# A hybrid decoder trunk on one core: squares summed on VectorE, 512-column query, key and output-gate products, and gate projections stacked into one fp32r pass

## The chip, the core and the metric

The program runs on one core of a Trainium2 chip. TensorE (PE) multiplies matrices and adds up in PSUM, VectorE (DVE) and ScalarE (ACT) do elementwise work, GpSimd (POOL) a little of it, and SyncE's queue (SP) issues the transfers. Each engine runs its own list of instructions in order and waits by semaphores. The metric is the device time of one execution in microseconds, as a median over runs.

## The reference, cut to what matters

The trunk has two layers on x of 256 tokens by 2048 channels: a convolution module and a feed-forward network (FFN), then gated linear attention and a second FFN. Around each of the four sub-layers stand an RMS norm, a modulation by a conditioning vector c (`w_ada`: six chunks of 2048 per layer) and a second RMS norm on its output. The change touches the attention and the place of some `w_ada` tiles:

```python
def gla_mixer(h, w_in, w_gate_up, b_gate, norm_g, w_out):
    proj = h @ w_in
    q, k, v, r, a = jnp.split(proj, [...])      # 1024, 1024, 2048, 2048, 16 columns
    g = jax.nn.log_sigmoid((a @ w_gate_up + b_gate).astype(jnp.float32)) / GLA_GATE_TAU
    ...
    _, o = lax.scan(step, S0, (qc, kc, vc, gc))  # chunks of 64 tokens, 4 heads
    o = rms_norm(o, norm_g.reshape(GLA_HEADS, GLA_HEAD_V))
    o = o.reshape(bsz, L, GLA_DV).astype(h.dtype) * jax.nn.silu(r)
    return o @ w_out
```

Each of the four heads has 256 columns of q and k and 512 of v and o. The norm of o takes the mean of squares over the 512 columns of one head and one token.

## The kernel before

Activations stand transposed, channels on the 128 partitions and tokens along the free dimension. A weight matrix is cut into 128x128 blocks. Sixteen blocks make a tile of 1 MB, which one transfer on SP's queue brings into a `raw` buffer (six of them, L321). Each half of a tile, eight blocks, is split: ScalarE casts it to fp32r as `hi` (L326), VectorE subtracts to get the rest, `lo` (L327). Three halves are prepared ahead of the one in use. A product of a block with an activation pair x_hi, x_lo is hi times x_hi, hi times x_lo and lo times x_hi. `product()` does this in three ways: "packed", two blocks in one bank, three matmuls of 256 columns (L368 to L370); "narrow", three of 256 columns into one half of a bank (L392, L393, L398); and wide, one of 512 columns over x_hi and x_lo side by side (L395) and one of 256 (L398). A wide result stands in two halves of a bank that have to be added: `joined` has ScalarE copy one (L410) and VectorE add the other (L411).

The order of tiles is a list (`tile_order`, L90): the weight tiles of the stages, with the tiles of `w_ada` spread among them. A `w_ada` tile, an "ada" tile below, goes through the same buffers, but VectorE alone uses it: one multiplication with a sum along the row over 128x2048 elements (L303). `EARLY` says how many ada tiles of one chunk, `scale2`, stand in the first FFN; the rest stand in the stages v, r and wo of the attention. Which instruction of an engine stands behind which is set by a scheduler at build time, from the order of the code and its own plan of times; the engines then keep to it.

Between two sub-layers stands a `junction` (L524): sums over channels by TensorE (`sum_sq`, L418: fp32, two passes per matmul, one result column, for each half of the tokens), then 1/sqrt on GpSimd and VectorE, a matmul that spreads it over the partitions, the new x, and the modulation into h. A few matmuls (`fill`) run in its pauses. The junction j1 leads from the first FFN into the attention. Its sums end with those of the last output block: f_y, f_z (squares on ScalarE) and f_xz (a product on VectorE, L515).

The attention (L823 to L982) has these stages:

- aqk: 17 blocks of columns: the 16 gate columns first (padded to 128), then q and k by head. The first eight are computed side by side ("packed", over half of the rows), the nine after that "narrow". When the gate block is done, `gates()` (L839) makes the decays: eight products z in fp32 from `wgu` (16x1024, loaded at L831) and `at` (16x256), each with an Abs on ScalarE (L845) and an addition with a minimum on VectorE (L846); then an Exp (L849) and a Ln (L850) over 128x2048, a subtraction on VectorE (L851), eight running sums (L853). After that `level`, `merge` and `diagonal` work off the scores by head, some in the v stage.
- v: the value columns.
- `attend(h)` (L947): per head four blocks of o (L953, L954). ScalarE squares each (L956), VectorE copies it (L957), and `sum_sq` adds it over channels on TensorE, into one result per head (`sso`). Then 1/sqrt, its spreading (`no_rb`), and the scaling of o.
- r: 16 narrow blocks. `r_done` takes silu, multiplies with o, splits into `oo`.
- wo: 16 blocks over `oo`, 15 of them wide; then the junction j2.

Of the kernel before, what the change touches and what calls it, by code (L numbers as in the profile page):

```python
# [7 lines left out]
F32 = mybir.dt.float32  # L8
F32R = mybir.dt.float32r
I8 = mybir.dt.int8  # L10
AF = mybir.ActivationFunctionType
ALU = mybir.AluOpType
PSUM = bass.MemoryType.PSUM

P = 128
D = 2048
KD = D // P
T = 256
# [6 lines left out]
DK = 1024  # L25
KK = DK // P
RANK = 16
EPS = 1e-6
HEAD = 8
TILE = 16  # L30
HALF = 8
LEAD = 8
EARLY = 4
CRITICAL = 3000
FILL = 8
TBUFS = 5
# [98 lines left out]
def trunk(ctx: ExitStack, tc: tile.TileContext, a: dict, out: bass.AP):  # L135
    nc = tc.nc
# [5 lines left out]
    tmp = ctx.enter_context(tc.tile_pool(name="tmp", bufs=2))  # L142
# [48 lines left out]
    inv_e = const.tile([P, 1], F32, tag="inv_e", name="inv_e")  # L191
# [7 lines left out]
    h = const.tile([P, KD, 2, T], F32R, tag="h", name="h")  # L199
    h_hi, h_lo = h[:, :, 0, :], h[:, :, 1, :]  # L200
    s_y = const.tile([P, T], F32, tag="s_y", name="s_y")
# [216 lines left out]
    def sum_sq(ssp, sq, w, first, last):  # L418
        for t in range(2):
            ends["sum"] = nc.tensor.matmul(  # L420
                ssp[:, t : t + 1], sq[:, t * P : (t + 1) * P], w,
                start=first and t == 0, stop=last, skip_group_check=True,
            ).ins

    def new_ss(name):
        return ps2.tile([P, 512], F32, tag="ss", name=name)
# [27 lines left out]
    def new_sq(name):  # L454
        return tmp.tile([P, T], F32, tag="sq", name=name, bufs=3)
# [22 lines left out]
    def square_into(total, src, name, first, **kw):  # L478
        if first:
            nc.scalar.activation(out=total, in_=src, func=AF.Square, **kw)  # L480
            return
        sq = new_sq(name)
        nc.scalar.activation(out=sq, in_=src, func=AF.Square, **kw)
        nc.vector.tensor_tensor(out=total, in0=total, in1=sq, op=ALU.add)
# [338 lines left out]
    with tc.tile_pool(name="gla", bufs=1) as gp:  # L823
# [3 lines left out]
        nc.gpsimd.memset(sc1, 0.0)  # L827
        vt = y.rearrange("p (t k) n -> p t (k n)", t=2)
        with tc.tile_pool(name="scores", bufs=1) as sp:
            wgu = sp.tile([RANK, DK], F32, tag="wgu", name="wgu")  # L830
            nc.sync.dma_start(out=wgu, in_=a["wgu"])  # L831
            at = sp.tile([P, T], F32, tag="at", name="at")
            bc = sp.tile([P, KK, T], F32, tag="bc", name="bc")
            gm = y[:, :KK, :]
            keep = sp.tile([P, T], F32, tag="keep", name="keep")
            nc.gpsimd.memset(keep, 1.0)
# [2 lines left out]
            def gates():  # L839
                nc.scalar.preload_act_table_set("natural_log_exp_and_others")  # L840
                for j in range(KK):
                    z = ps2.tile([P, 512], F32, tag="acc", name=f"z{j}", bufs=2)[:, :T]
                    nc.tensor.matmul(z, wgu[:, j * P : (j + 1) * P], at[:RANK, :], start=True, stop=True)
                    bg = col("gla_b_gate", j)
                    nc.scalar.activation(out=bc[:, j, :], in_=z, func=AF.Abs, bias=bg)  # L845
                    nc.vector.tensor_scalar(  # L846
                        out=gm[:, j, :], in0=z, scalar1=bg, scalar2=0.0, op0=ALU.add, op1=ALU.min
                    )
                nc.scalar.activation(out=bc, in_=bc, func=AF.Exp, scale=-1.0)  # L849
                nc.scalar.activation(out=bc, in_=bc, func=AF.Ln, bias=1.0)  # L850
                nc.vector.tensor_tensor(out=gm, in0=gm, in1=bc, op=ALU.subtract)  # L851
                for j in range(KK):
                    nc.vector.tensor_tensor_scan(  # L853
                        out=bc[:, j, :], data0=keep, data1=gm[:, j, :], initial=0.0, op0=ALU.mult, op1=ALU.add
                    )
# [36 lines left out]

            def aqk_done(ob, acc):
                if ob == 2 * KK:
                    nc.scalar.copy(at[:RANK, :], acc[:RANK, :])
                    gates()
                    return
                h = (ob % KK) // 2
                if h not in qk:
                    qk[h] = [  # L900
                        sp.tile([P, 2, T], F32, tag=tag, name=f"{tag}{h}", bufs=HEADS) for tag in ("q", "k")
                    ]
                which = ob // KK
                nc.scalar.activation(
                    out=qk[h][which][:, ob % 2, :], in_=acc, func=AF.Copy, scale=1.0 if which else 0.0625
                )
                if which and ob % 2:
                    work.extend((h, s) for s in (128, 64, 32, 16, 8, 4, 2, 1, 0))
# [7 lines left out]
                        else:  # L916
                            diagonal(h)

            product("aqk", KD, h_act, aqk_done, step, narrow=range(2 * KK + 1), packed=HEAD * KD)

            accs = {}
            for idx, (ob, k) in enumerate(ORDERS["v"]):
# [20 lines left out]
        with tc.tile_pool(name="og", bufs=1) as op:  # L943
            oo = op.tile([P, KD, 2, T], F32R, tag="oo", name="oo")
            on = {}

            def attend(h):  # L947
                ssp = new_ss(f"sso{h}")[:, :2]
                o = [op.tile([P, T], F32, tag="o", name=f"o{h}{j}", bufs=6) for j in range(4)]
                for j in range(4):  # L950
                    e = slice((4 * h + j) * P, (4 * h + j + 1) * P)
                    po = ps2.tile([P, 512], F32, tag="acc", name=f"po{h}{j}", bufs=2)[:, :T]
                    nc.tensor.matmul(po, vt[:, 0, e], sc0[:, h, :], start=True, stop=False)  # L953
                    nc.tensor.matmul(po[:, P:], vt[:, 1, e], sc1[:, h, :], start=False, stop=True)  # L954
                    sq = new_sq(f"o_sq{h}{j}")
                    nc.scalar.square(sq, po)  # L956
                    nc.vector.tensor_copy(o[j], po)  # L957
                    sum_sq(ssp, sq, inv_e, j == 0, j == 3)
                rbo = rstd(ssp, f"no{h}")
                for j in range(4):  # L960
                    nc.vector.scalar_tensor_tensor(
                        out=o[j], in0=o[j], scalar=col("gla_norm_g", 4 * h + j), in1=rbo,
                        op0=ALU.mult, op1=ALU.mult,
                    )
                on[h] = o

            def r_done(ob, acc):
                sr = tmp.tile([P, T], F32, tag="t", name=f"sr{ob}", bufs=TBUFS)
                nc.scalar.activation(out=sr, in_=acc, func=AF.Silu)
                nc.vector.tensor_tensor(out=sr, in0=sr, in1=on[ob // 4][ob % 4], op=ALU.mult)  # L970
                gather_x(ob, "w")
                split(sr, oo[:, ob, 0, :], oo[:, ob, 1, :])
                if ob % 4 == 1 and ob // 4 + 1 < HEADS:
                    attend(ob // 4 + 1)

            attend(0)
            product("r", KD, h_act, r_done, narrow=range(KD))

            def wo_done(ob, acc):
                gather(ob, "w", acc, kind=5)  # L980

            product("wo", KD, lambda k: oo[:, k, :, :], wo_done, narrow=(KD - 1,))  # L982
# [110 lines left out]
```

## Time and profile before

| | before |
|---|---|
| median of 3 runs | 2414.77 us (2414.39 to 2417.88) |
| profiled execution | 2412.25 us |
| its span, first to last instruction | 2410.5 us |
| mean granted TensorE clock (share of full) | 0.986 |
| busy: TensorE / its weight loads / VectorE / ScalarE / GpSimd | 98% / 85% / 73% / 46% / 1% |
| moved from and to the chip's memory | 605.27 MB, 251 GB/s on average |

The span begins with the first instruction of the program and ends with the last; the execution's time is 1.75 us longer. Times in the trace count from the span's start. The first FFN runs from about 452 to 1194 us, the junction j1 to 1206, aqk to 1325, v to 1437, r to 1545, wo to 1634, the junction j2 to 1647. Matmuls are pipelined, so that the durations of neighbours overlap. What one costs is read from start to start, or from the number of matmuls in a window that they fill.

### The profile page before, as it was taken

How to read it: one execution, taken by the hardware profiler on the slowest of the kernel's cores; microseconds unless marked ns; L12 is line 12 of the kernel's file. 1: busy time of each engine (PE TensorE's matmuls, PEld its weight loads, DVE VectorE, ACT ScalarE, POOL GpSimd, SP SyncE). 2: the span in 40 equal slices, each digit the busy share in tenths (PEclk: the TensorE clock that was granted, in tenths of full speed). 3: DMA queues.
4: the chain of work that ended last, by engine and by line, in shares of the span. 5: the costliest groups of instructions: out<-in, count | busy, mean ns of one | idle time of the engine just before them, and what ended most of it. 6: DMA issues, size and time to landing. Idle time of an engine off the chain costs nothing.

```text
span 2410.5 us, 36312 instructions
## 1 busy us (share of the span) xinstructions
PE 2353.3 (98%) x14672; PEld 2051.8 (85%) x14672; DVE 1763.6 (73%) x2490; ACT 1110.1 (46%) x1659; POOL 23.9 (1%) x27
## 2 busy tenths in 40 slices
PE   7899999999999999999999999999999999999997
PEld 4677688998888888888899889989888888888886
DVE  5776669887776687779877978898666555666665
ACT  4333345554444444444455444454444444444442
POOL 0000000000000000000000000000000000000001
PEclk8999999999999999999999999999999999999998
DMA  9987978368777788778743666774565665665651
GB/s 390 392 341 277 345 272 336 134 244 300 287 286 285 290 307 293 292 283 295 269 158 127 245 253 252 283 274 140 204 216 209 222 217 208 224 214 208 223 184 65
DMA packets 85027, 605.27 MB, mean 251 GB/s; under 512 B 9574, under 2 KB 9958, under 8 KB 12022
## 3 DMA queue, kind: packets, MB, share of 16 engines
q1 hardware_dynamic: 84858, 602.95, 68.6%
q8 instruction: 115, 1.88, 0.3%
q14 instruction: 54, 0.43, 0.0%
HBM read 600.81 MB, written 2.10 MB: 250 GB/s over the span
## 4 chain that ended last, share of the span: by engine, by line
PE 94%; DVE 2%; DMA 2%; ACT 1%; issue 1%; POOL 0%; SPq 0%; POOLq 0%; ACTq 0%
PE in L395 25%; PE out L395 13%; PE in L398 12%; PE out L398 7%; PE pw L729 3%; PE pw L724 3%; PE pw L730 2%; PE wo L395 2%; PE r L392 1%; PE r L393 1%; PE r L398 1%; PE in_pair L369 1%; PE wo L398 1%; PE in_pair L368 1%; PE in_pair L370 1%; PE v L934 1%
## 5 line engine op out<-in xcount | busy, mean ns | idle before, releaser
L327 DVE TENSOR_TENSOR lo<-raw,hi 128x1024 fp32r<-128x1024 f32 x754 | 920.5, 1223 | 520.5 <-ACT hi L326 515.8
L326 ACT CAST hi<-raw 128x1024 fp32r<-128x1024 f32 x754 | 790.3, 1050 | 1048.9 <-issue 295.0
L395 PE MATMUL in<-h,hi 128*128 128x512 f32 x2560 | 900.1, 398 | 0.1
L398 PE MATMUL in<-h,lo 128*128 128x256 f32 x2560 | 716.7, 280 | 0.0
L395 PEld LDWEIGHTS in<-h,hi 128*128 128x128 f32 x2560 | 481.0, 188 | 117.8 <-DVE gate L799 0.3
L398 PEld LDWEIGHTS in<-h,lo 128*128 128x128 f32 x2560 | 483.4, 189 | 0.0
L395 PE MATMUL out<-m,hi 128*128 128x512 f32 x1364 | 477.3, 395 | 0.0
L398 PE MATMUL out<-m,lo 128*128 128x256 f32 x1408 | 392.2, 281 | 0.0
L303 DVE SCALAR_TENSOR_TENSOR raw<-raw,cb 128x2048 f32<-128x2048 f32 x160 | 365.2, 2284 | 12.1 <-DMA raw<-in_w_ada_dram 12.0
L395 PEld LDWEIGHTS out<-m,hi 128*128 128x128 f32 x1364 | 255.0, 188 | 58.4
L398 PEld LDWEIGHTS out<-m,lo 128*128 128x128 f32 x1408 | 264.4, 188 | 1.9
L724 PE MATMUL pw<-hi,h 128*128 128x512 f32 x256 | 101.3, 417 | 7.0 <-ACT h L467 6.7
L729 PE MATMUL pw<-lo,h 128*128 128x512 f32 x256 | 106.2, 417 | 1.2 <-DVE lo L327 1.2
L730 PE MATMUL pw<-hi,h 128*128 128x512 f32 x256 | 94.0, 395 | 0.0
L395 PE MATMUL wo<-oo,hi 128*128 128x512 f32 x240 | 83.7, 394 | 0.0
L398 PE MATMUL r<-h,lo 128*128 128x256 f32 x256 | 73.3, 286 | 0.0
L392 PE MATMUL r<-h,hi 128*128 128x256 f32 x256 | 73.2, 286 | 0.0
L393 PE MATMUL r<-h,hi 128*128 128x256 f32 x256 | 73.0, 285 | 0.0
L398 PE MATMUL wo<-oo,lo 128*128 128x256 f32 x256 | 71.2, 281 | 0.0
L369 PE MATMUL in_pair<-h,hi 128*128 128x256 f32 x256 | 70.9, 284 | 0.0
L370 PE MATMUL in_pair<-h,lo 128*128 128x256 f32 x256 | 68.9, 283 | 0.0
L368 PE MATMUL in_pair<-h,hi 128*128 128x256 f32 x256 | 68.0, 284 | 0.0
(363 smaller groups left out, 2939.1 us busy)
## 6 DMA issues: line engine op xcount, KB each, us to landing
raw<-in_in_dram SPq DMA_DIRECT2D x176, 1024.0 KB, 5.0
raw<-in_w_ada_dram SPq DMA_DIRECT2D x160, 1024.0 KB, 5.2
raw<-in_out_dram SPq DMA_DIRECT2D x88, 1024.0 KB, 5.0
raw<-in_pw_dram SPq DMA_DIRECT2D x48, 1024.0 KB, 7.7
raw<-in_w_ada_r_dram SPq DMA_DIRECT2D x32, 1024.0 KB, 8.3
raw<-in_aqk_dram SPq DMA_DIRECT2D x17, 1024.0 KB, 5.1
raw<-in_v_dram SPq DMA_DIRECT2D x16, 1024.0 KB, 5.0
raw<-in_r_dram SPq DMA_DIRECT2D x16, 1024.0 KB, 6.6
```

Source lines behind the costliest of these rows:

```text
L303: nc.vector.scalar_tensor_tensor(out=raw, in0=raw, scalar=1.0, in1=cb, op0=ALU.mult, op1=ALU.mult, accum_out=modcol(name, i))
L326: nc.scalar.copy(hi, part)
L327: done = nc.vector.tensor_tensor(out=lo, in0=part, in1=hi.bitcast(F32), op=ALU.subtract)
L369: nc.tensor.matmul(acc, w_hi, x_lo, start=False, stop=False, skip_group_check=True)
L370: nc.tensor.matmul(acc, w_lo, x_hi, start=False, stop=closes, skip_group_check=True)
L392: nc.tensor.matmul(acc[:, :T], w_hi[:, s], x_hi, start=n == 0, stop=False)
L393: nc.tensor.matmul(acc[:, :T], w_hi[:, s], x_lo, start=False, stop=False)
L395: nc.tensor.matmul(acc, w_hi[:, s], pair.rearrange("p a b -> p (a b)"), start=n == 0, stop=end, skip_group_check=True)
L398: nc.tensor.matmul(acc[:, :T], w_lo[:, s], x_hi, start=False, stop=end, skip_group_check=ob not in narrow)
L724: nc.tensor.matmul(accs[c][t], h_hi[:, k, n], w_hi[:, s], start=k == 0, stop=False)
L729: nc.tensor.matmul(accs[c][t], h_hi[:, k, n], w_lo[:, s], start=False, stop=False)
L730: nc.tensor.matmul(accs[c][t], h_lo[:, k, n], w_hi[:, s], start=False, stop=k == KD - 1)
```

## The change

There are four parts.

1. `EARLY` goes from 4 to 12: eight ada tiles move from the stages v, r and wo into the first FFN.
2. The gate projection's operands are stacked. `wgu` has 96 rows: the 16 rows of the weight stand at rows 0, 32 and 64, zeros between. They come by a transfer of 384 KB into the memory of `bc`, ScalarE casts all to fp32r, VectorE replaces the last group by the rest. The gate block of aqk has its columns three times, so `at` has 96 rows, of which the second group is replaced by its rest. One fp32r matmul over 96 rows then adds hi times hi, hi times rest and rest times hi.
3. aqk (the nine blocks that are not packed) and r lose `narrow`: they are wide, and joined. `sr` takes the place of the joined tile.
4. In `attend` the squares of a head's four blocks are added in `s_y` or `s_z` by `square_into` (a Square on ScalarE and, after the first, an add on VectorE), and one `sum_sq` per head follows.

```diff
-EARLY = 4
+GATE_ROWS = 32
+GATE_K = 3 * GATE_ROWS
+EARLY = 12
...
-            wgu = sp.tile([RANK, DK], F32, tag="wgu", name="wgu")
-            nc.sync.dma_start(out=wgu, in_=a["wgu"])
-            at = sp.tile([P, T], F32, tag="at", name="at")
             bc = sp.tile([P, KK, T], F32, tag="bc", name="bc")
+            gate_up = bc[:GATE_K, :, :].rearrange("p a b -> p (a b)")[:, :DK]
+            nc.sync.dma_start(out=gate_up, in_=a["wgu"])
+            wgu = sp.tile([GATE_K, DK], F32R, tag="wgu", name="wgu")
+            nc.scalar.copy(wgu, gate_up)
+            low = slice(2 * GATE_ROWS, GATE_K)
+            nc.vector.tensor_tensor(out=wgu[low, :], in0=gate_up[low, :], in1=wgu[low, :].bitcast(F32), op=ALU.subtract)
+            at = sp.tile([GATE_K, T], F32R, tag="at", name="at")
...
-                    nc.tensor.matmul(z, wgu[:, j * P : (j + 1) * P], at[:RANK, :], start=True, stop=True)
+                    nc.tensor.matmul(z, wgu[:, j * P : (j + 1) * P], at, start=True, stop=True)
...
-                    nc.scalar.copy(at[:RANK, :], acc[:RANK, :])
+                    nc.scalar.copy(at, acc[:GATE_K, :])
+                    low = slice(GATE_ROWS, 2 * GATE_ROWS)
+                    nc.vector.tensor_tensor(out=at[low, :], in0=acc[low, :], in1=at[low, :].bitcast(F32), op=ALU.subtract)
                     gates()
...
-            product("aqk", KD, h_act, aqk_done, step, narrow=range(2 * KK + 1), packed=HEAD * KD)
+            product("aqk", KD, h_act, aqk_done, step, packed=HEAD * KD)
...
             def attend(h):
-                ssp = new_ss(f"sso{h}")[:, :2]
+                total = (s_y, s_z)[h % 2]
...
-                    sq = new_sq(f"o_sq{h}{j}")
-                    nc.scalar.square(sq, po)
+                    square_into(total, po, f"o_sq{h}{j}", j == 0)
                     nc.vector.tensor_copy(o[j], po)
-                    sum_sq(ssp, sq, inv_e, j == 0, j == 3)
+                ssp = new_ss(f"sso{h}")[:, :2]
+                sum_sq(ssp, total, inv_e, True, True)
...
-                sr = tmp.tile([P, T], F32, tag="t", name=f"sr{ob}", bufs=TBUFS)
+                sr = acc
...
-            product("r", KD, h_act, r_done, narrow=range(KD))
+            product("r", KD, h_act, r_done)
...
-    aqk[:, 2 * DK : 2 * DK + RANK] = w_in[:, 2 * DK + 2 * D :]
+    gate_up = np.zeros((GATE_K, DK), w_in.dtype)
+    for at in range(0, GATE_K, GATE_ROWS):
+        aqk[:, 2 * DK + at : 2 * DK + at + RANK] = w_in[:, 2 * DK + 2 * D :]
+        gate_up[at : at + RANK] = f["gla_w_gate_up"][0]
```

Two lines more stand at the top of the changed kernel, so that a line there has a number two higher up to the attention. VectorE in the junction j1, before: j_r and f_xz belong to its chain, lo is the rest of a weight half.

```order
L327 TENSOR_TENSOR lo_10550<-raw_10547,hi_10549 128x1024
L508 TENSOR_SCALAR y<-y,der 128x256
L535 TENSOR_SCALAR j_r_10606<-j_my 128x2
L515 TENSOR_TENSOR f_xz_10585<-y,x 128x256
L435 TENSOR_TENSOR j1y_dg<-ident,j1y_r_10608 128x256
```

VectorE at the same place of the changed kernel:

```order
L329 TENSOR_TENSOR lo_10574<-raw_10571,hi_10573 128x1024
L523 TENSOR_TENSOR s_xz<-s_xz,f_xz_10522 128x256
L510 TENSOR_SCALAR y<-y,der 128x256
L537 TENSOR_SCALAR j_r_10630<-j_my 128x2
L838 TENSOR_TENSOR wgu<-bc,wgu 32x1024
L517 TENSOR_TENSOR f_xz_10609<-y,x 128x256
L437 TENSOR_TENSOR j1y_dg<-ident,j1y_r_10632 128x256
```

The subtraction of the gate weights (L838) now stands between j_r and f_xz. ScalarE there, in the changed kernel:

```order
L328 CAST hi_10573<-raw_10571 128x1024
L504 ACTIVATE f_y_10606<-y 128x256
L836 CAST wgu<-bc 96x1024
L521 ACTIVATE f_z_10611<-y 128x256
L482 ACTIVATE s_xx<-x 128x256
```

The cast of the gate weights (L836) stands between f_y and f_z, which were neighbours. VectorE in the gate chain of aqk, before: L851 is the subtraction after the logarithm, L853 the eight running sums.

```order
L327 TENSOR_TENSOR lo_11416<-raw_11413,hi_11415 128x1024
L327 TENSOR_TENSOR lo_11420<-raw_11413,hi_11419 128x1024
L851 TENSOR_TENSOR y<-y,bc 128x2048
L327 TENSOR_TENSOR lo_11491<-raw_11488,hi_11490 128x1024
L853 SCALAR_TENSOR_TENSOR bc<-keep,y 128x256 x8
L327 TENSOR_TENSOR lo_11495<-raw_11488,hi_11494 128x1024
```

The same place of the changed kernel:

```order
L329 TENSOR_TENSOR lo_11544<-raw_11541,hi_11543 128x1024
L413 TENSOR_TENSOR join_12_11567<-aqk_11524,join_12_11567 128x256
L857 TENSOR_TENSOR y<-y,bc 128x2048
L329 TENSOR_TENSOR lo_11548<-raw_11541,hi_11547 128x1024
L329 TENSOR_TENSOR lo_11604<-raw_11601,hi_11603 128x1024
L859 SCALAR_TENSOR_TENSOR bc<-keep,y 128x256 x8
L413 TENSOR_TENSOR join_13_11627<-aqk_11584,join_13_11627 128x256
L329 TENSOR_TENSOR lo_11608<-raw_11601,hi_11607 128x1024
```

One rest of a weight half has moved from ahead of the subtraction to behind it, and joins stand between.

## Rows read from the trace of the kernel before

**Rows 1.** Page, section 4: the chain that ended last, by engine.

```profile
PE 94%; DVE 2%; DMA 2%; ACT 1%; issue 1%; POOL 0%; SPq 0%; POOLq 0%; ACTq 0%
```

**Rows 2.** Windows (aqk, r, wo, FFN0): length, busy us of PE, PEld, DVE, ACT, POOL; PEclk; DMA, GB/s.

```profile
1253.50:1325.50 72.00, 69.14 (x538) 65.84 (x538) 53.89 (x96) 41.45 (x72) 0.00 (x0) 0.98 0.39 132
...
1436.70:1544.60 107.90, 107.90 (x883) 107.09 (x882) 88.95 (x139) 53.43 (x92) 4.14 (x4) 1.00 0.71 260
1544.60:1634.40 89.80, 89.80 (x533) 79.29 (x531) 81.29 (x132) 47.32 (x78) 0.00 (x0) 1.00 0.75 272
452.00:1190.00 738.00, 737.93 (x4347) 649.66 (x4346) 587.37 (x748) 350.24 (x506) 0.00 (x0) 1.00 0.78 283
```

**Rows 3.** Groups by line and shape: busy us, mean ns of one, idle before.

```profile
L327 DVE TENSOR_TENSOR lo<-raw,hi 128x1024 fp32r<-128x1024 f32 x754 | 920.5, 1223 | 520.5 <-ACT hi L326 515.8 <-PE ada L255 2.7
L326 ACT CAST hi<-raw 128x1024 fp32r<-128x1024 f32 x754 | 790.3, 1050 | 1048.9 <-issue 295.0 <-PE in L395 240.6 <-PE out L395 227.6
L303 DVE SCALAR_TENSOR_TENSOR raw<-raw,cb 128x2048 f32<-128x2048 f32 x160 | 365.2, 2284 | 12.1 <-DMA raw<-in_w_ada_dram 12.0
...
L411 DVE TENSOR_TENSOR join<-in,join 128x256 f32<-128x256 f32 x160 | 66.7, 417 | 0.0
...
L420 PE MATMUL sso<-inv_e,o_sq 128*128 128x1 f32 x64 | 7.8, 235 | 0.0
```

**Rows 4.** Short windows: steady r, steady wo, then aqk behind its longest wait.

```profile
1520.00:1540.00 20.00, 20.00 (x168) 19.95 (x167) 17.34 (x22) 9.27 (x14) 0.00 (x0) 1.00 0.74 269
1560.00:1580.00 20.00, 20.00 (x116) 17.47 (x115) 19.25 (x29) 10.72 (x18) 0.00 (x0) 1.00 0.90 331
...
1289.50:1292.90 3.40, 3.40 (x18) 3.40 (x18) 3.40 (x6) 1.97 (x6) 0.00 (x0) 0.50 0.68 280
1293.00:1296.40 3.40, 3.40 (x30) 3.40 (x30) 2.55 (x6) 1.60 (x3) 0.00 (x0) 1.00 0.89 301
```

**Rows 5.** Timeline of TensorE at a z product: start us, us, engine, line, work.

```profile
1262.78 0.28 PE L398 MATMUL aqk<-h,lo 128*128 128x256 f32 x1
1262.99 0.69 PE L843 MATMUL z<-at,wgu 16*128 16x256 f32 x2
1263.61 0.39 PE L392 MATMUL aqk<-h,hi 128*128 128x256 f32 x1
1263.83 0.28 PE L393 MATMUL aqk<-h,hi 128*128 128x256 f32 x1
```

**Rows 6.** Timeline of TensorE around eight passes of a head's sums.

```profile
1453.53 0.95 PE L420 MATMUL sso<-inv_e,o_sq 128*128 128x1 f32 x8
1454.34 0.36 PE L393 MATMUL r<-h,hi 128*128 128x256 f32 x1
1454.54 0.28 PE L398 MATMUL r<-h,lo 128*128 128x256 f32 x1
```

**Rows 7.** Timeline of the junction j1, all engines.

```profile
1194.55 0.33 SPq L831 DMA_DIRECT2D wgu<-in_wgu_dram  x1
...
1197.08 0.43 DVE L515 TENSOR_TENSOR f_xz<-y,x 128x256 f32<-128x256 f32 x1
...
1197.57 1.01 PE L420 MATMUL j_m<-two_d,f_xz 128*128 128x1 f32 x4 [1.06 <-DVE f_xz L515]
```

**Rows 8.** Transfers: count, KB each, median us from issue to landing.

```profile
out_dram<-x SPq DMA_DIRECT2D x8, 256.0 KB, 2.0
...
wgu<-in_wgu_dram SPq DMA_DIRECT2D x1, 64.0 KB, 4.8
```

**Rows 9.** Timeline of VectorE in the gate chain.

```profile
1278.99 2.29 DVE L851 TENSOR_TENSOR y<-y,bc 128x2048 f32<-128x2048 f32 x1 [2.00 <-ACT bc L850]
...
1282.33 4.76 DVE L853 TENSOR_TENSOR_SCAN bc<-keep,y 128x256 f32<-128x256 f32 x8
```

**Rows 10.** Timeline of TensorE there: the two waits.

```profile
1282.47 0.39 PE L398 MATMUL aqk<-h,lo 128*128 128x256 f32 x1 [0.44 <-DVE lo L327]
...
1288.26 0.39 PE L398 MATMUL aqk<-h,lo 128*128 128x256 f32 x1 [2.43 <-DVE lo L327]
```

More of the change, by code (lines that the diff above doesn't have):

```diff
@@ L1075 @@
     arr["wo"] = tiles(f["gla_w_out"][0], "wo")
-    arr["wgu"] = np.ascontiguousarray(f["gla_w_gate_up"][0])
+    arr["wgu"] = gate_up
     for l in range(2):
```

## The prediction

> **What bounds the kernel now.** I read the chain of waits first: TensorE holds 94% of the chain that ended last [rows 1]. So only time that TensorE loses or is given can move the end, and other engines count where TensorE waits for them. Next the windows by stage [rows 2]: the reader is to see that the matmuls fill the r, wo and FFN0 stages to the last 0.1 us, and that only aqk has idle time on TensorE, 72.00 - 69.14 = 2.86 us. The short windows [rows 4] give the pitch, which is the window over the number of matmuls: a matmul row's own duration (0.28 us in the timeline) overlaps the next one's and is no cost. The timelines then give the price of the small matmuls between the weight products [rows 5, 6], the end of FFN0, where TensorE has nothing else to do [rows 7], and the gate chain, where it waits for VectorE [rows 9, 10].
>
> **Wide products for aqk and r.** 9 aqk blocks and 16 r blocks of 16 products each, 25 x 16 = 400 pairs, change from three 256-column matmuls to one of 512 columns and one of 256. Three narrow ones take 3 x 20.00/168 = 0.357 us, a wide pair 2 x 20.00/116 = 0.345 [rows 4]; the difference is 0.012. Over the whole wo stage the pair comes to 0.350 (89.80 less 48 narrow matmuls at 0.119, over 240 pairs [rows 2]), against the 0.360 that the steady pitch of 0.12 gives [rows 5]: 0.010. I take 0.011, so 4.4 us, with bounds of 0.009 and 0.014 a pair: 3.6 to 5.6. The joins that this adds (an ACT copy and a VectorE add of 0.417 us per block [rows 3]) lie beside matmuls, apart from the two places below.
> The Trainium skill, "TensorE: Matmul & The Clock Gate", Back-to-back issue gap, speaks against this term: its isolated gap for a full clock is N/2.4 + 2.5 ns, so an estimate from it is three narrow at 109 ns = 328 against 216 + 109 = 325 ns, and the sum would gain 1.1 us here instead of 4.4. The trace does not agree: the narrow matmul's 0.119 us lies above that gap and the pair's 0.345 lies 0.012 below three of them.
>
> **Gate projections.** Eight z products of two passes each become one fp32r pass of 256 columns with 96 rows. Today a z holds TensorE from 1262.99 to 1263.61, 0.62 us, and the matmul before it and the one after it take 0.21 and 0.22 to the next start where 0.12 is normal [rows 5]. If a pass of 0.12 replaces only the 0.62, 0.50 is saved; if both slow starts go too, 0.69. I take 0.54, near the lower end since another shape is loaded either way: 8 x 0.54 = 4.3 us (4.0 to 5.5).
>
> **Squares summed on VectorE.** Sixteen sum pairs of two passes each, 64 passes [rows 3], become four, 16 passes. Eight passes take 1453.53 to 1454.34, 0.81 us, and the next matmul starts slow, 0.2 us [rows 6]: 0.101 to 0.115 a pass. At 0.108 the 48 passes that go are worth 5.2 us (4.8 to 5.5). VectorE gets 12 adds of 0.417.
>
> **What it costs at the end of FFN0.** The order of VectorE and ScalarE puts the new cast and subtraction of the gate weights into the chain of the junction: the subtraction stands ahead of f_xz, for which TensorE waits (1.06 us idle before j_m [rows 7]). Nothing covers TensorE there. The transfer is issued at about 1194.5 as now (it waits for the tiles of FFN0). A 256 KB transfer takes 2.0 us to land [rows 8]; 128 KB more at the 283 GB/s of FFN0 [rows 2] is 0.46, so it lands at about 1197.0. Then the cast, 1.05, and a subtraction as long as one of 1024 columns, 1.22 [rows 3], with some 0.1 between: f_xz starts at 1199.35 where it started at 1197.08, +2.3 us. The bounds are a landing 0.6 earlier (+1.7) and one after 4.8 us, as the 64 KB transfer had today [rows 8] (+4.6). On SP the seventh aqk tile now stands behind this transfer; six are ahead of it, and at 16 x 0.357 = 5.7 us each it is not used until some 34 us after the stage begins, so its delay costs nothing; were it late, its price would be its delay less those 34.
>
> **The gate chain.** Today TensorE is idle 0.44 and 2.43 us for lo tiles behind the log-sigmoid subtraction (2.29) and the eight scans (4.76) [rows 9, 10]; that is the 2.86 of the stage. After it runs at half clock: 18 matmuls in the 3.4 us where 30 go at full [rows 4], 12 x 0.113 = 1.4 us. The new order has one lo, a join, the subtraction, two lo, the scans, a join, a lo. One lo feeds 8 pairs, 2.8 us, and the next product's first matmul (0.2) needs no lo. From the first lo's end to the second's: 0.42 + w + 2.29 + 1.22, where w is what the subtraction waits for the logarithm; less 3.0 that is 0.9 + w. From the second's to the fourth's: 1.22 + 4.76 + 0.42 + 1.22 = 7.6, less two feeds, 5.8: 1.8. Together 2.7 + w against 2.9 now. w is 2.00 today [rows 9], behind one lo more, but with z sooner; I take 0.5: +0.3. Bounds: all stalls gone, -2.9, and w near 3, +3; the half clock may go (-1.4) or come twice (+1.4). The new 32-row subtraction for `at` (about 0.4) delays z, not TensorE, which has aqk blocks to work on.
>
> **Starts of r and wo.** Head 0's attention moves from the end of v into r, and its result is needed by the first r block's product. The row of its scaling stands five halves into r, so I take +0.5 for some late VectorE work (0 to 2.5, the length of one gate-sized wait [rows 10]). The last oo tile comes a copy, a join and some of an ada later, about 1.5 us; the first wo block's last product has some nine instructions of the second block ahead of it, 9 x 0.172 = 1.6: +0.5 (0 to 2).
>
> **Eight ada tiles to FFN0.** 8 x 2.284 = 18.3 us of VectorE [rows 3] move to a stage where it is busy 587.37 of 738.00 and TensorE is full [rows 2]: 0.82 afterwards. I take 0; at worst each holds up one lo, 8 x 1.22 = 9.8; nothing can be gained there, nor in r and wo, where TensorE does not wait now. In r, VectorE gets 16 joins and 12 adds, 28 x 0.417 = 11.7, and loses about four ada tiles, 9.1: the cover of the joins stays.
>
> **Sum.** 4.4 + 4.3 + 5.2 = 13.9 gained; 2.3 + 0.3 + 0.5 + 0.5 = 3.6 lost; net 10.3. The profiled execution took 2412.25 us (span 2410.5), so 2401.95 by its time; it lies 2.5 below the median of 2414.77, against which the forecast stands: 2404.5.
>
> **Rivals.**
> A, the sum above, 2404.5, its own range 2401 to 2407.5.
> B, the waits eat more: the gate weights land after 4.8 us (+4.6) and the gate chain waits with w near 3 and a second half-clock stretch (+4.4). 13.9 - 4.6 - 4.4 - 1.0 leaves 3.9: 2410.9, in milder forms from 2408, with late r and wo starts as well 2413. For it: VectorE is the releaser in both stalls today [rows 10]. Against: a 256 KB transfer landed in 2.0.
> C, slower: VectorE becomes what paces r. The stage wants 107.90 - 2.8 - 5.2 = 99.9 us, VectorE has 88.95 + 2.6 = 91.6 of work in it, a share of 0.917. It decides from the share at which lo tiles come late. If VectorE, waiting for casts, can't be over today's 0.824 [rows 2], r takes 111.1, 3.2 longer than before; the rest, 5.9 gained (13.9 - 8.0) and 3.6 lost, leaves 2415.7, and if waits in each of the four heads bring a half-clock stretch of 1.4 us, 2421. Against: in wo VectorE is busy 0.905 of the stage and 19.25 of 20.00 us in one window, with TensorE full [rows 2, 4].
> D, better: the reordered gate chain lets lo tiles run ahead, and the stalls and the half clock go (-4.3), with r and wo on time: 13.9 - 2.3 + 4.3 = 15.9: 2398.9. For it: two lo stand together between subtraction and scans.
> E, the wide operand does nothing: columns and not instructions set the pitch, a pair costs what three narrow matmuls cost. 13.9 - 4.4 - 3.6 = 5.9: 2408.9. For it: in r a pair has 768 columns either way. Against: the two pitches of [rows 4]. By the page's figures above it would be 2407.8.
>
> **Chances.** A 0.50, B 0.22, C 0.07, D 0.17, E 0.04. No change is within 0.2%, 4.8 us, about what a measurement of this kernel can tell: 2409.9 to 2419.6. Faster: A, D, three quarters of E and a third of B, 0.77. Within: the rest of B and E, 0.16. C I put wholly to slower, 0.07. The range 2400 to 2411 holds A, E, half of D and two thirds of B.
>
> **What would show it.** The r window per pair at 0.345 to 0.350 with VectorE near 0.92 and no wait of TensorE (A, against C and E); z matmuls without the 0.62; 16 sum passes for the heads; f_xz 2 to 3 us later against the last FFN0 matmul; and the gate chain's waits at about 3 us. I am wrong if r's matmuls wait for lo, if f_xz is over 4 us late, or if FFN0 is longer than its 738 us.

## The result, and the profile after

The changed kernel takes 2400.68 us (median of 4 runs, 2395.94 to 2404.08) where the kernel before takes 2415.51 in the same session: the ratio is 0.9936 with a 95% interval of 0.9916 to 0.9956. Between the medians that is 14.8 us less. Measured again in another session (e1 below) it is 2401.16 against 2413.82, ratio 0.9949 (0.9935 to 0.9962). The forecast was 2404.5, 10.3 below the median it started from, with a range of 2400 to 2411 and a chance of 0.77 for faster.

The profiled execution took 2395.94 us, 16.31 less than that of before. Where that lies is read from the starts of the matmuls that open and close each stage. FFN0 and FFN1 are the first and the second FFN, j1 and j2 the junctions in front of aqk and behind wo:

| us | before | after | difference |
|---|---|---|---|
| to the first matmul of FFN0 | 452.32 | 451.86 | -0.46 |
| FFN0 | 741.92 | 741.71 | -0.21 |
| junction j1 | 11.83 | 15.34 | +3.51 |
| aqk, v, r, wo | 428.06 | 414.58 | -13.48 |
| junction j2 | 13.30 | 11.99 | -1.31 |
| FFN1 | 745.37 | 741.51 | -3.86 |
| rest | 17.69 | 17.17 | -0.52 |

The terms of the sum lie in j1 and in aqk to wo: -9.97 against the -10.3 forecast. The forecast did not speak of the two others with a size, FFN1 and j2. Inside aqk to wo, the time from each matmul's start to the next one's start (its pitch), added up by tile, changed by these amounts: aqk -4.3, z -3.8, sums of squares (`sso`) -4.7, r -2.8, v +0.6, wo +1.5.

The chain that ended last, after the change, for [rows 1]: TensorE still binds, VectorE has one percent more.

```profile
PE 93%; DVE 3%; DMA 2%; ACT 1%; issue 1%; POOL 0%; SPq 0%; POOLq 0%; ACTq 0%; DVEq 0%
```

The windows after for [rows 2]: aqk from its first block that is not packed, r, wo, FFN0; the columns are those of [rows 2].

```profile
1255.20:1313.40 58.20, 55.73 (x326) 48.05 (x325) 42.10 (x64) 38.99 (x64) 0.00 (x0) 1.00 0.48 166
1430.00:1532.20 102.20, 102.20 (x594) 90.05 (x593) 90.86 (x159) 58.30 (x109) 4.03 (x4) 1.00 0.66 242
1532.30:1623.50 91.20, 90.42 (x532) 79.19 (x531) 79.29 (x135) 48.37 (x81) 0.00 (x0) 1.00 0.67 247
452.00:1190.00 738.00, 737.93 (x4348) 649.64 (x4348) 602.75 (x760) 349.81 (x505) 0.00 (x0) 1.00 0.79 295
```

r keeps TensorE full with VectorE at 90.86 of 102.20, 0.89, so rival C is out. wo has 0.78 us of idle time that it did not have before. FFN0 carries its extra ada tiles (VectorE 602.75, where the forecast adds up to 605.7) without a loss.

The junction after, which answers to [rows 7]: start, duration, engine, line.

```profile
1193.88 0.33 SPq L834 DMA_DIRECT2D bc<-in_wgu_dram  x1
...
1197.62 1.04 ACT L836 CAST wgu<-bc 96x1024 fp32r<-96x1024 f32 x1 [2.46 <-DMA bc<-in_wgu_dram]
...
1198.70 1.22 DVE L838 TENSOR_TENSOR wgu<-bc,wgu 32x1024 fp32r<-32x1024 f32 x1 [1.96 <-ACT wgu L836]
1199.95 0.43 DVE L517 TENSOR_TENSOR f_xz<-y,x 128x256 f32<-128x256 f32 x1
...
1200.43 1.01 PE L422 MATMUL j_m<-two_d,f_xz 128*128 128x1 f32 x4 [2.33 <-DVE f_xz L517]
```

It takes 3.74 us from the issue of the transfer to the cast's start. Then come cast, subtraction and f_xz, one behind the other, as the forecast had them. f_xz starts 6.38 us after the last matmul of FFN0 (at 1193.57); before the change it was 2.84. That is +3.5 where +2.3 was forecast.

A z product after, for [rows 5], and the sums of one head, for [rows 6]:

```profile
1258.48 0.40 PE L397 MATMUL aqk<-h,hi 128*128 128x512 f32 x1
1258.72 0.40 PE L849 MATMUL z<-at,wgu 96*128 96x256 f32 x2
1258.96 0.28 PE L400 MATMUL aqk<-h,lo 128*128 128x256 f32 x1
...
1443.76 0.50 PE L422 MATMUL sso<-inv_e,s_y 128*128 128x1 f32 x4
```

Two z (`x2` merges two neighbours in one row) take 0.24 us together, and no slow start stands beside them. The four passes of `sso` are all that a head's sums take now.

The gate chain on VectorE after, for [rows 9], and the waits of TensorE, for [rows 10]:

```profile
1285.72 2.29 DVE L857 TENSOR_TENSOR y<-y,bc 128x2048 f32<-128x2048 f32 x1 [1.93 <-ACT bc L856]
1287.93 2.35 DVE L329 TENSOR_TENSOR lo<-raw,hi 128x1024 fp32r<-128x1024 f32 x2
1290.20 4.76 DVE L859 TENSOR_TENSOR_SCAN bc<-keep,y 128x256 f32<-128x256 f32 x8
1294.88 0.40 DVE L413 TENSOR_TENSOR join<-aqk,join 128x256 f32<-128x256 f32 x1
1295.20 1.22 DVE L329 TENSOR_TENSOR lo<-raw,hi 128x1024 fp32r<-128x1024 f32 x1
```

```profile
1287.94 0.50 PE L397 MATMUL aqk<-h,hi 128*128 128x512 f32 x1 [0.18 <-ACT hi L328]
1289.21 0.39 PE L400 MATMUL aqk<-h,lo 128*128 128x256 f32 x1 [0.77 <-DVE lo L329]
...
1296.47 0.39 PE L400 MATMUL aqk<-h,lo 128*128 128x256 f32 x1 [1.43 <-DVE lo L329]
```

TensorE is idle 2.38 us here, before 2.87, but in shorter pieces: two lo tiles now stand between the subtraction and the scans, where one stood. And the half clock of [rows 4] is gone (granted clock 1.00):

```profile
1294.80:1298.20 3.40, 1.97 (x12) 1.55 (x11) 3.40 (x7) 2.86 (x4) 0.00 (x0) 1.00 0.21 39
1298.20:1301.60 3.40, 3.31 (x19) 2.65 (x18) 3.40 (x7) 3.26 (x9) 0.00 (x0) 1.00 0.65 275
```

### The profile page after: what moved, and what is told of

The parts are those of the page before. It is cut to its first block, busy times and chain, and to the rows that moved or that the text cites. A ratio compares the mean times of both kernels' runs of the same rounds, so it can differ in the third digit from the quotient of the medians.

```text
span 2394.2 us, 35471 instructions
## 1 busy us (share of the span) xinstructions
PE 2337.7 (98%) x14216; PEld 2021.1 (84%) x14216; DVE 1775.1 (74%) x2529; ACT 1116.5 (47%) x1685; POOL 23.7 (1%) x27
## 4 chain that ended last, share of the span: by engine, by line
PE 93%; DVE 3%; DMA 2%; ACT 1%; issue 1%; POOL 0%; SPq 0%; POOLq 0%; ACTq 0%; DVEq 0%
PE in L397 25%; PE out L397 13%; PE in L400 12%; PE out L400 7%; PE pw L731 3%; PE r L397 2%; PE pw L726 2%; PE wo L397 2%; PE pw L732 2%; PE r L400 1%; PE in_pair L371 1%; PE wo L400 1%; PE in_pair L370 1%; PE in_pair L372 1%; PE v L941 1%; PE v L942 1%
## 5 line engine op out<-in xcount | busy, mean ns | idle before, releaser
L397 PE MATMUL r<-h,hi 128*128 128x512 f32 x256 | 90.9, 397 | 0.0
L413 DVE TENSOR_TENSOR join<-in,join 128x256 f32<-128x256 f32 x160 | 66.9, 418 | 0.0
```

Of the source, the lines that this page charges most:

```text
L397: nc.tensor.matmul(acc, w_hi[:, s], pair.rearrange("p a b -> p (a b)"), start=n == 0, stop=end, skip_group_check=True)
L413: nc.vector.tensor_tensor(out=dst, in0=acc[:, :T], in1=dst, op=ALU.add)
```

## The experiments

Two questions were open. Which parts of the change pay? The stages agreed with the sum but hardly with its terms (aqk gained 4.3, not 1.3; wo lost 1.5, not 0.5). And did FFN1, whose instructions the change does not touch, become faster by it? The theory was the sum of the prediction, with chance in FFN1. The rivals were that the wide operand is worth nothing, that the ada tiles, put at 0, are worth something, and that the change makes FFN1 faster.

Medians of the same kernel differ by some us between sessions, and the time to the first convolution matmul alone runs from 339.8 to 346.3 in these profiles, whatever the kernel. So the stages of the profiles are the sharper measure here: each line is one profile, in us from matmul start to matmul start, and "sum" adds the three stages. The ratios come from all runs of a session, so they differ a little from the quotients of the medians named below.

| kernel | j1 | aqk to wo | j2 | sum | ratio to before (95%) |
|---|---|---|---|---|---|
| before | 11.83 | 428.06 | 13.30 | 453.19 | |
| before, again (e7) | 11.60 | 428.08 | 14.94 | 454.62 | 1.0007 (0.9996 to 1.0018) |
| changed | 15.34 | 414.58 | 11.99 | 441.91 | 0.9936 (0.9916 to 0.9956) |
| changed, again (e1) | 15.64 | 414.43 | 10.52 | 440.59 | 0.9949 (0.9935 to 0.9962) |
| e2: aqk, r narrow | 15.23 | 415.69 | 11.53 | 442.45 | 0.9948 (0.9935 to 0.9960) |
| e3: EARLY 4 | 12.40 | 420.94 | 12.05 | 445.39 | 0.9960 (0.9943 to 0.9976) |
| e12: narrow, EARLY 4 | 12.46 | 415.14 | 13.31 | 440.91 | 0.9952 (0.9934 to 0.9970) |
| e5: gate in fp32 | 12.40 | 419.68 | 10.50 | 442.58 | 0.9939 (0.9919 to 0.9960) |
| e6: sums per block | 15.24 | 419.67 | 10.51 | 445.42 | 0.9946 (0.9931 to 0.9961) |
| e4: gate weights behind j1 | 10.77 | 414.56 | 11.76 | 437.09 | 0.9935 (0.9922 to 0.9947) |
| e4 again (e9) | 12.40 | 414.57 | 11.78 | 438.75 | 0.9920 (0.9904 to 0.9936) |
| e8: e4, aqk narrow | 10.78 | 414.05 | 11.74 | 436.57 | 0.9925 (0.9908 to 0.9942) |
| e10: e8, EARLY 16 | 13.41 | 413.11 | 10.51 | 437.03 | 0.9940 (0.9927 to 0.9954) |
| e11: before, EARLY 12 | 10.77 | 428.89 | 10.52 | 450.18 | 0.9979 (0.9970 to 0.9988) |

"aqk to wo" repeats within 0.15 us for the same kernel; j1 and j2 only within some 1.6. With them the granted clock differs: for the same program it was on average 0.84 in j1 of e4 and 0.72 in e9, and 0.72 and 0.84 in j2 of the changed kernel's two profiles. So a difference of 1.6 us in a junction's length tells nothing of a change.

**e1 and e7, both kernels again, no edit.**

> The changed kernel again, unaltered. Theory 1 (the sum of the prediction, and chance in the second FFN): its median is 10 to 14 us below the kernel before, and the time from the first matmul of the second FFN to its last (745.4 us in the profile of before, 741.5 in that of after) comes out anywhere from 741 to 746 in another profile of the same kernel, because pairs there go at 0.353 us in some executions and at 0.346 in others. Theory 2 (the change makes the second FFN faster): 741.5 again, within 0.5.

> The kernel before, unaltered, for a second profile. Theory 1 (chance in the second FFN): its first FFN (741.9 us from first to last matmul in the first profile) and its second (745.4) come out anywhere from 741 to 746. Theory 2 (the kernel decides): 741.9 and 745.4 again, within 0.5.

FFN1 took 741.53 us in e1 and 745.14 in e7, as in the first profiles of each. That is what theory 2 expected, by which the kernel decides.

**e4, the gate weights' work behind the junction, and e9, the same again.**

```diff
-        nc.scalar.activation(out=h_hi[:, k, :], in_=t, func=AF.Identity, bias=sh)
+        ends["h_hi"] = nc.scalar.activation(out=h_hi[:, k, :], in_=t, func=AF.Identity, bias=sh).ins
...
-            nc.scalar.copy(wgu, gate_up)
-            nc.vector.tensor_tensor(out=wgu[low, :], in0=gate_up[low, :], ...)
+            with tc.issue_after(ends["h_hi"]):
+                nc.scalar.copy(wgu, gate_up)
+            with tc.issue_after(gate[0]):
+                nc.vector.tensor_tensor(out=wgu[low, :], in0=gate_up[low, :], ...)
```

> The changed kernel with the cast and the subtraction of the gate weights ordered behind the junction's last modulation instead of into its chain; the same work, the same transfer. If they cost 3.5 us in the junction (f_xz 6.4 us after the last matmul of the first FFN against 2.8 before), it is 3.5 us faster than the changed kernel and f_xz stands 2.8 to 3.0 us after that matmul. If the junction has another bound beside it, or the moved work holds up weight halves in aqk, 0 to 1.5.

> The kernel with the gate weights' work behind the junction, unaltered, for a second profile. Its second FFN took 745.4 us in the first. If its pitch is a matter of the execution, it may be 741.5 now; if the kernel decides, 745.4 again. The stages from the first aqk matmul to the last wo matmul: 414.6 us again, within 0.3, either way.

e4 takes 2397.71 us against 2401.16 for the changed kernel in the same session, 3.45 less. Its junction shows f_xz 3.1 us after the last FFN0 matmul (1197.96), with TensorE not waiting for it:

```profile
1201.10 0.43 DVE L517 TENSOR_TENSOR f_xz<-y,x 128x256 f32<-128x256 f32 x1
...
1201.77 0.58 PE L422 MATMUL j_m<-two_d,f_xz 128*128 128x1 f32 x4
```

The moved work costs nothing where it stands now (aqk to wo 414.56 against 414.58), and j1 is 10.77 us in e4 and 12.40 in e9 against 15.34 and 15.64 with the work in the junction. So the junction term is real and was undersized.

The same two runs bear on FFN1: it took 745.36 us in e4 and 741.54 in e9, with the same program. FFN1 works through the products `in_pair`, `in`, `out`, `in` and `out`. One stretch of the first `in` product in both, first e4, then e9:

```profile
1750.00:1850.00 100.00, 100.00 (x569) 86.66 (x568) 61.60 (x78) 47.64 (x72) 0.00 (x0) 1.00 0.61 220
```

```profile
1750.00:1850.00 100.00, 100.00 (x579) 88.17 (x578) 61.41 (x77) 48.26 (x72) 0.00 (x0) 1.00 0.60 217
```

569 matmuls against 579 in 100 us, at the full granted clock, are a pair every 0.353 or 0.347 us (from start to start over 64 pairs, 0.3533 and 0.3467). The whole product of 576 pairs took 203.52 us in e4 and 199.68 in e9. So an execution can decide at which of the two pitches a product runs.

But the kernel before and the changed one do not differ in this product (203.52 and 203.51). They differ in the second `in` product, 704 pairs, 248.74 against 244.06. One stretch of it before the change, after it, in e4 and in e9:

```profile
2060.00:2160.00 100.00, 100.00 (x568) 86.69 (x568) 61.89 (x77) 47.16 (x71) 0.00 (x0) 1.00 0.60 208
```

```profile
2060.00:2160.00 100.00, 100.00 (x579) 87.43 (x578) 63.53 (x79) 48.38 (x73) 0.00 (x0) 1.00 0.62 221
```

```profile
2060.00:2160.00 100.00, 100.00 (x568) 86.73 (x568) 62.05 (x77) 47.95 (x72) 0.00 (x0) 1.00 0.61 221
```

```profile
2060.00:2160.00 100.00, 100.00 (x567) 86.76 (x566) 63.20 (x78) 47.10 (x71) 0.00 (x0) 1.00 0.60 220
```

Here both profiles of one kernel agree each time: before and e7 are slow, the changed kernel and e1 fast, e4 and e9 slow. Of the others, e2, e6 and e8 are fast, e3, e5, e10, e11 and e12 slow. In this product no kernel changed its pitch from one profile to the other, so chance is not shown to have made the 3.86 us of FFN1. Nor is the change: e4 and e9 contain it and are slow, and in FFN1 the operations and tiles of TensorE, VectorE and ScalarE stand in the same order before, after and in e4. What brings these 3.86 us of the profile's 16.31 stays open.

**e2, narrow again.**

```diff
-            product("aqk", KD, h_act, aqk_done, step, packed=HEAD * KD)
+            product("aqk", KD, h_act, aqk_done, step, narrow=range(2 * KK + 1), packed=HEAD * KD)
...
-                sr = acc
+                sr = tmp.tile([P, T], F32, tag="t", name=f"sr{ob}", bufs=TBUFS)
...
-            product("r", KD, h_act, r_done)
+            product("r", KD, h_act, r_done, narrow=range(KD))
```

> The changed kernel with aqk and r narrow again (three 256-column matmuls, no join), the rest as changed. If a wide pair is 0.011 us shorter than three narrow matmuls, it is 4.4 us slower than the changed kernel (3.6 to 5.6), of which 2.8 lies in r; the joins that go may give back up to 2 in the gate chain. If the wide operand does nothing (rival E), the two are equal within 1 us.

The medians are equal, 2401.47 against 2401.16. By stages it loses 1.11 us from aqk to wo. The matmuls of r take 2.75 us more, 256 pairs at 0.0107, the forecast price. But aqk takes only 0.5 more: with wide blocks the pitch in the gate chain is 2.97 us above normal, with narrow ones 1.87, where no join stands between the scans and the next lo on VectorE. The two waits left:

```profile
1288.01 0.39 PE L400 MATMUL aqk<-h,lo 128*128 128x256 f32 x1 [0.65 <-DVE lo L329]
...
1294.93 0.39 PE L400 MATMUL aqk<-h,lo 128*128 128x256 f32 x1 [0.91 <-DVE lo L329]
```

The matmuls of v take 0.9 less and those of wo 0.9 less. So the pair is cheaper, as forecast, and three quarters of the gain is given back.

**e3, EARLY 4 in the changed kernel; e12, EARLY 4 and narrow; e11, EARLY 12 in the kernel before.** The edits are `EARLY = 12` to `EARLY = 4` (in e12 with the edit of e2), and `EARLY = 4` to `EARLY = 12` in the kernel before.

> The changed kernel with EARLY at 4, so that the eight w_ada tiles stay in v, r and wo. The prediction's term is 0: within 1 us of the changed kernel, the first FFN 741.6 us in both. Rival: VectorE is near its limit in v, r and wo once the joins are there, and eight tiles of 2.28 us more hold up weight halves: waits of TensorE for lo appear in v, r or wo and the three stages are 2 to 9 us longer than the changed kernel's 320.4 from the first v matmul to the last wo matmul plus 0.1 (v 114.98 + 1.45, r 102.23, wo 91.16).

> The changed kernel with narrow aqk and r and EARLY at 4: only the gate projection and the sums changed. If the 5.6 us that wo lost with EARLY at 4 came from the pile-up of joins behind w_ada tiles on VectorE, wo is 89.5 to 91.2 us here. If the order of the tiles alone does it, 96.7 again.

> The kernel before with EARLY at 12 and nothing else. If the move of eight tiles pays only where the new joins and adds load VectorE, its stages from the first aqk matmul to the last wo matmul are 428.1 us as before, within 0.5. If the tiles cost time in v, r and wo by themselves, some 6 us less.

e3 loses 6.36 us from aqk to wo, and its median is 2406.97. wo takes 96.7 us instead of 91.2. The longest wait in wo in its timeline, VectorE and then TensorE, and the window behind it:

```profile
1590.62 2.28 DVE L305 SCALAR_TENSOR_TENSOR raw<-raw,cb 128x2048 f32<-128x2048 f32 x1
...
1593.17 0.42 DVE L413 TENSOR_TENSOR join<-wo,join 128x256 f32<-128x256 f32 x1
```

```profile
1593.73 0.60 PE L397 MATMUL wo<-oo,hi 128*128 128x512 f32 x1 [2.53 <-DVE join L413]
```

```profile
1593.70:1597.10 3.40, 3.37 (x11) 2.90 (x12) 3.38 (x9) 1.02 (x3) 0.00 (x0) 0.53 1.02 407
```

An ada tile stands ahead of a join; TensorE waits for the join 2.53 us, and then runs at half clock. In e12, with narrow blocks in aqk and r (wo is wide in both), the same EARLY gives wo 89.5 us, no such wait, and 415.14 from aqk to wo. So the ada tiles together with the joins of aqk and r are what costs. VectorE makes TensorE wait, as in rival C, but mostly in wo (5.7 us by the pitch of its matmuls) and little in r (1.1), and the move of the tiles is what kept it away in the changed kernel. e11 agrees for aqk to wo (428.89 against 428.06: no gain there), but its median is 3.4 us below that of before (2410.78 against 2414.20), and in its profile j2 is shorter, 10.52 us against 13.30 and 14.94. The trace of before has a wait there that stands in none of the rows ahead of the prediction. e11, second, has another order of the sums and a shorter wait:

```profile
1637.02 0.61 PE L420 MATMUL j_my<-inv_d,s_y 128*128 128x1 f32 x4 [2.27 <-DVE s_y L484]
```

```profile
1643.76 0.38 PE L420 MATMUL j_m<-two_d,w_xz 128*128 128x1 f32 x2 [1.01 <-DVE w_xz L515]
```

That is 1.3 of the 2.8 us. The rest goes with the clock: on average 0.74 was granted in j2 before and 0.84 in e11, and the changed kernel's two profiles differ as much (0.72 and 0.84, 11.99 and 10.52 us, with the same wait of 1.2). The short wait does not need the move of the tiles either: e3, with EARLY 4 and wide blocks, has 1.00, and e12, with EARLY 4 and narrow ones, 2.27.

That j1 takes 12.4 us in e3 and e12 has its own reason: with EARLY 4 the scheduler puts the cast and the subtraction behind f_xz (which starts 2.84 us after FFN0, as before). So the loss of 3.5 in j1 came from the new gate operands and EARLY 12 together.

**e5, the gate projection of before.**

```diff
-            wgu = sp.tile([GATE_K, DK], F32R, tag="wgu", name="wgu")
+            wgu = sp.tile([RANK, DK], F32, tag="wgu", name="wgu")
+            nc.sync.dma_start(out=wgu, in_=a["wgu"][:RANK, :])
...
-                    nc.tensor.matmul(z, wgu[:, j * P : (j + 1) * P], at, start=True, stop=True)
+                    nc.tensor.matmul(z, wgu[:, j * P : (j + 1) * P], at[:RANK, :], start=True, stop=True)
```

The cast and both subtractions, of `wgu` and of `at`, go with it.

> The changed kernel with the gate projection of before: 16 rows of wgu, fp32 z products in two passes, no cast and no subtractions. By the traces z takes 4.80 us of pitch instead of 0.96, and the slow starts next to it some 1.5 more; the junction gets its 3.5 us back. Theory 1 (these are all): 1.5 to 2.5 us slower than the changed kernel by the stages up to wo. Rival: the half clock after the gate chain comes back too, because z makes the chain later against the weight halves: 1.4 us more, 3 to 4.

It takes 5.10 us more from aqk to wo, and 2.9 less in j1. z is 3.26 of the loss (4.22 against 0.96), the aqk matmuls 2.40. One lo alone stands between subtraction and scans on VectorE, one wait is long again, and the clock behind it is half:

```profile
1289.19 1.22 DVE L329 TENSOR_TENSOR lo<-raw,hi 128x1024 fp32r<-128x1024 f32 x1
1290.32 0.42 DVE L413 TENSOR_TENSOR join<-aqk,join 128x256 f32<-128x256 f32 x1
1290.66 4.76 DVE L855 TENSOR_TENSOR_SCAN bc<-keep,y 128x256 f32<-128x256 f32 x8
```

```profile
1296.58 0.58 PE L400 MATMUL aqk<-h,lo 128*128 128x256 f32 x1 [2.84 <-DVE lo L329]
```

```profile
1296.60:1300.00 3.40, 3.40 (x11) 2.96 (x12) 3.40 (x6) 1.95 (x6) 0.00 (x0) 0.52 0.70 231
```

So the stacked pass also took away the long wait and the half clock: the rival's reading, against the first theory's. All profiles agree: with fp32 z (before, e5, e7, e11) one lo stands there and a wait of 2.41 to 2.84 us follows, with the stacked pass two stand there and no wait in the chain is over 1.44. The median of the whole kernel, 2402.48 us, tells nothing here; the stages do.

**e6, one sum per block on TensorE.**

```diff
-                total = (s_y, s_z)[h % 2]
+                ssp = new_ss(f"sso{h}")[:, :2]
...
-                    square_into(total, po, f"o_sq{h}{j}", j == 0)
+                    sq = new_sq(f"o_sq{h}{j}")
+                    nc.scalar.square(sq, po)
...
-                ssp = new_ss(f"sso{h}")[:, :2]
-                sum_sq(ssp, total, inv_e, True, True)
+                    sum_sq(ssp, sq, inv_e, j == 0, j == 3)
```

> The changed kernel with one sum on TensorE per block again (64 passes instead of 16) and no adds of squares on VectorE. If the passes are what they cost, r and the end of v are 4.7 us longer (6.16 against 1.45 us of pitch), up to 5.5 with slow starts. If the 12 adds on VectorE and the later 1/sqrt cost something that now goes, 1 to 3 less.

It takes 5.09 us more from aqk to wo, 4.85 of it in the passes themselves (6.30 against 1.45). The term of 5.2 holds, and the 12 adds cost nothing that shows. By its median (2401.97) it can't be told from the changed kernel.

**e8 and e10, towards a better kernel.** e8 is e4 with aqk narrow and r wide; e10 is e8 with `EARLY = 16`.

> The gate weights' cast and subtraction behind the junction, aqk narrow again, r wide. The kernel with narrow aqk and narrow r lost 2.75 us in r and gained 0.9 in v and 0.9 in wo. If the gain in v belongs to narrow aqk (its nine joins stand in VectorE's way where the scores begin), this kernel is 0.5 us faster than the one with only the move (v stage 111.2 instead of 115.0, aqk up by less), and about 16 us below the kernel before; if wide aqk is worth its own 1.6 us, it is 1 to 1.6 slower. The second FFN's 741.5 or 745.4 may come out either way; a difference from that is none of the edit's.

> Gate weights behind the junction, aqk narrow, r wide, and EARLY at 16: four more w_ada tiles in the first FFN. If VectorE still costs time in r or wo, these get up to 1.2 us shorter (the two waits of 0.48 and 0.72 at the start of wo). If those waits belong to the order of TensorE alone, it equals the kernel with 12 within 0.3, and the first FFN stays at 741.6.

e8 has 414.05 from aqk to wo, 0.5 less than e4, as expected if v's time belongs to aqk's joins: from its first to its last matmul v is back at 111.2 us. e10 takes 0.9 more off, and the two waits early in wo are gone, 0.32 and 0.46 us of idle time some 15 us after its first matmul. They ended with a cast on ScalarE; that four ada tiles fewer removed them is shown, by which path is not. The median of e8 is 2398.62 (ratio 0.9925), that of e10 2401.50. In e10's profile the second `in` product of FFN0 ran at the slower pitch (FFN0 746.8 us, in all others 741.4 to 742.2), so its median does not tell how it compares with e8. e4 is 3.45 us below the changed kernel in one session, and e4, e8 and e9 (ratios 0.9920 to 0.9935) lie below its 0.9936 and 0.9949, with intervals that overlap; by the stages they are 2 to 5 us shorter. Which of them is best stays open.

## Why the prediction was right in its sum, and where it was wrong in its terms

The median of 2400.68 lies 0.7 us inside the range and just under rival A's own (2401 to 2407.5).

- **Wide pairs, 4.4 us: wrong as a gain of the stages.** The pair's price was right (0.0107 in r against 0.011). The step that the joins "lie beside matmuls, apart from the two places below" failed: they cost TensorE 1.1 us in the gate chain and 0.9 in wo, which lie near the two places named, and 0.9 in v, which was not named. What remains is 1.1 us (e2), and for aqk alone it is a loss of 0.5 (e8). The Trainium skill ("TensorE: Matmul & The Clock Gate", Back-to-back issue gap) gives an isolated gap of N/2.4 + 2.5 ns, by which the 400 pairs would be worth 1.0 us, an estimate (2.5 ns a pair; the prediction, from rounded terms, had 1.1). The trace does not agree with its reason: in r the pair itself is 0.0107 us shorter.
- **Gate projections, 4.3 us: about right for z, too small for what hangs on it.** z's own pitch gave 3.84, just under the bounds of 4.0 to 5.5; the slow starts beside it are counted with aqk's matmuls. The step that failed was the gate chain's +0.3, beside which "the half clock may go (-1.4) or come twice (+1.4)" was left in the bounds: the long wait went, and with it the half clock. So of the two gains of rival D one came; the other, an end of the stalls, did not, since 2.38 us of shorter waits stayed. In the sum of the chain two errors stood against each other. The wait w for the logarithm was put at 0.5 and was 1.93. But TensorE waited only 0.95 us (0.18 and 0.77) in the step priced 0.9 + w: it went on for 4.1 us after the first lo's end, not 3.0. The second step, priced 1.8, took 1.43. The gate part is worth 5.1 us from aqk to wo when taken out of the changed kernel (e5), and 7.8 in narrow surroundings (before to e12, 12.9, less the 5.1 of the sums, if these are worth the same there), where 4.0 were forecast with the chain.
- **Sums on VectorE, 5.2 us: right**, 5.1 (e6), 0.101 a pass. (Its upper bound should have been 0.111 a pass by [rows 6], not 0.115.)
- **Junction, +2.3 us: right mechanism, wrong size**, +3.5. The cast began 3.7 us after the transfer's issue, inside the bounds of 1.9 and 4.8; scaling the 256 KB row gave 2.5.
- **Eight ada tiles, 0: wrong twice.** Alone they bring the median down by 3.4 us (e11). The prediction said that nothing can be gained where TensorE does not wait, and did not look at the start of j2, where TensorE waited 2.27 us; 1.3 of that went in e11, and the rest of the 3.4 has no shown cause. And where the joins are, the move keeps TensorE from waiting, which the prediction put at nothing: without it aqk to wo takes 6.4 us more, most of that in wo (e3).
- **Starts of r and wo, +1.0:** wo has two waits some 15 us after its first matmul, 0.48 and 0.72 us above pitch, and loses 1.5 in all; at r nothing shows.

One part after the other, from aqk to wo: gate and sums -12.92 (before to e12), the ada tiles +0.55 (e12 to e2), wide pairs -1.11 (e2 to changed), -13.48 together; with j1's +3.51 it is -9.97 against -10.3. That the sum came so near is luck in part: a gain put too large (wide) and a cost put too small (j1) stood against a gain put too small (the gate part). In the profile j2 gives another 1.3 us, of the size by which it differs for one kernel, and FFN1 3.86. Neither stands in the forecast. FFN1 is of the size of what is left of the 14.8 us between the medians; that the medians contain just this was not shown, nor that the change brings it.

e12 sums it up: with the gate projection and the sums alone, it takes 440.91 us from FFN0 to FFN1, against 441.91 and 440.59 with all four parts.

## What to carry to other kernels

Price a cheaper matmul together with what it adds on the engine that feeds TensorE: here a join of 0.42 us per block on VectorE was enough to give back three quarters of 4.4 us. For a short one-time preparation (weights cast for a later stage), look where the order puts it: in the junction here, where TensorE had nothing else to do, its transfer and both its steps cost 3.5 us, and behind the junction nothing. Undo the parts of a change one by one, in pairs too, and read stages, not totals: e2, e5 and e6 all looked like the changed kernel by their medians, and two of them were 5 us longer from aqk to wo. And when two executions of one program differ, look whether they differ in the same stretch as the two kernels do: e4 and e9 differ in another product than before and after.

## What the runs showed of the hardware

The same loop on the same operands runs at one of two pitches at the full granted clock, 0.3467 or 0.3533 us a pair, for a whole product of 576 or 704 pairs. Which one can differ between executions of one program (the first `in` product of FFN1 in e4 and e9, 3.84 us). In the second `in` product, where before and after differ by 4.68 us, the two profiles of each of three kernels agree. What decides it was not found: granted clock, VectorE's and ScalarE's load and the order of the instructions are alike.

TensorE's granted clock fell to half (0.50 to 0.53 in the windows shown) behind waits of 2.43 us [rows 10], 2.53 (e3) and 2.84 (e5) in otherwise full stages, and did not behind those of 0.77 and 1.43 (after); from aqk to wo the other profiles agree, with 2.41 and 2.42 in e7 and e11 and none above 1.44 in the rest. In the 3.4 us behind the long waits 11 wide matmuls went (e3, e5), or 18 narrow ones [rows 4], where about 20 or 30 go at the full clock. So a long wait costs more than itself, and two shorter ones with nearly the same sum did not.
